# One pool of equal rooms in place of pools by phase, in a two-layer decoder trunk

## The chip, the core and the metric

The kernel runs on one core of a Trainium2 chip. The metric is the time of one execution in microseconds (us) on the device. TensorE (PE) multiplies matrices, VectorE (DVE), ScalarE (ACT) and GpSimd (POOL) work element by element, SyncE (SP) starts most DMA transfers. PE writes to eight PSUM banks of 512 float32 columns, which DVE and ACT empty.

## The reference

An input x of 1024 tokens by 1024 features goes through two layers and a last norm. In each layer:

- u = rms_norm(h), and one projection of u gives q, k, v and a forget logit for 8 attention heads of 64, and q, k, v and a gate for 8 retention heads.
- Attention: softmax of q k / 8 plus the differences of a running sum of log-sigmoid forget logits, causal, times v.
- Retention: rotary q and k, in chunks of 128 tokens with a decaying state, then a norm for each head, times silu of the gate.
- h += concat(attention, retention) @ w_out.
- h += (gelu(conv3(rms_norm(h) @ w_up_a)) * (rms_norm(h) @ w_up_g)) @ w_down, with 2816 inner features.
- h += sigmoid(rms_norm(h) @ w_gate) * (p @ w_proj).

## The kernel before

All activations lie with features on the 128 partitions and the 1024 tokens along the free axis, so a tile is 128 x 1024 float32, 4 KB a partition. To keep float32 accuracy each operand is cut into a high and a low part (`split`, lines 111 to 117: a ScalarE cast and a subtraction on VectorE or GpSimd), and every product is three matmuls.

The program builder traces instructions in program order; a scheduler then orders each engine's queue by a simulated time, program order being the priority. So matmuls of different products may be mixed wherever their inputs are ready in the simulation. On the chip each queue runs in its order.

**Attention stage** (lines 758 to 898). Weights come through `load_w` (load, cast, subtract) with two buffers for each of its three tiles; `weights()` always fetches one more before it hands one out, so two are ahead. `weave` (line 843) mixes a chain of dense projections (`DENSE`) with units of attention and retention head pairs, each paced between two positions of the dense chain (`SPANS`). The last retention pair is paced between 251.1 and 259.3, over the embedding's projection (`g_embed`), the last of the chain. Each retention pair leaves two `turn`s (transposes into `mixed`) for later; those of the last pair come behind the weave.

**Matrix stages** (lines 901 to 1032). The out-projection, the up- and down-projection and the gate use a seven-product scheme for a 2 x 2 block product: `parts` (line 334) runs the products b0, a, b1, c1, b2, c2, b3 with three matmuls of 512 columns for each moving pair. b0, b1, b2 and b3 gather in one PSUM bank, c1 and c2 in another, a in a third, and between products of one bank the bank is read (`join`, `form`). `Moving` (line 215) holds the moving side of a pair of tiles in seven tiles: its sums and their splits. `Fixed` (line 259) holds the weight side, built in four steps beside the part before. A stage's norm is not applied ahead: `Stats` adds up squares, `finish` sums them with 16 small matmuls (line 404) and spreads the result with matmuls of line 418, and the result scales the products.

Phases follow each other through `turn_to`, which closes all tile pools of a phase and opens those of the next; a few tiles (`mh`, `ssq`, `rc`, `rb`) live across. In the matrix phase a tag has a fixed number of buffers: `mh` 9, `c` 2, `x` 28, `wr` 4, `ws` 2, `wh` 4, `wl` 3, and all 8 banks are one ring. Borders that matter here:

- All four `Moving` of the mixed heads are built at the start of the matrix phase (line 925), after all attention and retention. The out-projection has two halves of four `parts`, first on attention heads, then on retention heads; in the second half the u of the next stage is built from each finished pair of h (line 936).
- Up to down: the results z and their sums go to DRAM (`zd`), since all come back in groups of three or two (`GROUPS`). The reloaded tiles `zz` use two buffers of tag `c` and one of `mh` (lines 986 to 998).
- In the gate, tiles `sg` use the two buffers of `c`; each is last used as the room for a square (line 1031). Behind it layer 1 opens its pools, fetches two weights and builds eight u (lines 1034 to 1037).
- The last layer's gate runs in a stage of its own (lines 1039 to 1091), with u built at line 1042.

Of the kernel before, what the change touches and what calls it, by code (L numbers as in the profile page):

```python
# [17 lines left out]
DEPTH = 2  # L18
D = 1024
T = 1024  # L20
# [11 lines left out]
FVW = 264  # L32


DENSE = ("fi1", "fi2", "fv1", "fi3", "rv0", "ri0", "rv1", "rg0", "ri1", "ri2", "rg1", "ri3", "ep0", "em0")
SPANS = ((6, 42.6), (42.6, 79.9), (85.9, 123.5), (130.4, 145.5), (138.9, 199.2), (194.7, 197.7), (217.3, 254.5), (251.1, 259.3))

TURNS = (1, 2)
PIECES = ((0, 512), (512, 512))
# [21 lines left out]

@with_exitstack
def trunk(ctx, tc, ap):
    nc = tc.nc
    const = ctx.enter_context(tc.tile_pool(name="const", bufs=1))
    keep = ctx.enter_context(tc.tile_pool(name="keep", bufs=1))
    dr = ctx.enter_context(tc.tile_pool(name="dr", bufs=2, space=DRAM))

# [4 lines left out]
    BUFS = dict(st=6, tp=5, L=4, c=2, u=16, mh=9, ssq=1, x=28, wr=4, ws=2, wh=4, wl=3)  # L73
    KEPT = ("mh", "ssq")
    sb = ps = banks = None

    @contextmanager
    def phase(name):

        nonlocal sb, ps, banks  # L80
        banks = 8 if name[:3] == "ffn" else 4
        with ExitStack() as stack:
            sb = stack.enter_context(tc.tile_pool(name="sb_" + name, bufs=1, reuse_waits="tile"))
            ps = stack.enter_context(tc.tile_pool(name="ps_" + name, bufs=1, space=PSUM, reuse_waits="tile"))
            yield

    def G(tag, name, dt=F32, shape=(P, T)):
        return (keep if tag in KEPT else sb).tile(list(shape), dt, name=name, tag=tag, bufs=BUFS[tag])

# [3 lines left out]
    def spsum():  # L93
        return ps.tile([P, 512], F32, name="s", tag="s", bufs=banks)

    def bank():
        return ps.tile([P, 512], F32, name="q", tag="s", bufs=banks)

    def hb(name, dt=F32):
        return sb.tile([P, 512], dt, name=name, tag="hb", bufs=6)  # L100

    def small(name, shape, dt=F32, bufs=2):
        return (keep if name == "rc" else sb).tile(list(shape), dt, name=name, tag=name, bufs=bufs)
# [16 lines left out]
    def load_w(src, kk, width, eng):  # L120
        raw = sb.tile([P, kk, width], F32, name="wr", tag="wr", bufs=2)
        nc.sync.dma_start(raw, src)
        hi = sb.tile([P, kk, width], F32R, name="wh", tag="wh", bufs=2)
        lo = sb.tile([P, kk, width], F32R, name="wl", tag="wl", bufs=2)
        split(hi, lo, raw, eng)
        return hi, lo

    def weight_order():
        V, G_ = nc.vector, nc.gpsimd
        for l in range(DEPTH):  # L130
            qk = lambda j: (ap["wqk"][l, j], KC, P, E("qk", j))
            tm = lambda j: [(ap["wtm"][l, j, i], 4, 256, E("tm", 2 * j + i)) for i in range(2)]
            fv0 = [(ap["wfv"][l][i], 4, FVW, G_) for i in range(2)]
            specs = {"ep": lambda i: [],
# [6 lines left out]
            yield from (None, None)  # L141
# [11 lines left out]
    def weights():  # L153
        fetch()
        return ahead.pop(0)
# [30 lines left out]
    def g_dense_tm(x, evac):  # L186
# [3 lines left out]
        for i in range(2):  # L190
            hi, lo = weights()
# [9 lines left out]
    def dense_tm_wide(x, width, evac):  # L201
        w0 = weights()
        w1 = weights()
        for b in range(NB):
            if b % 2 == 0:
                d = dpsum()
            o = d[:, (b % 2) * 512:(b % 2) * 512 + width]
            for k in range(KC):
                hi, lo = (w0, w1)[k // 4]
                mm_tm(o, x, b, k, hi[:, k % 4, :], lo[:, k % 4, :], k == 0, k == KC - 1)  # L210
            evac(b, o)

    class Moving:


        def __init__(self, a, b, scales=None, ta=None, tb=None):

            a1, b1, b2 = a[:, 0:512], b[:, 0:512], b[:, 512:T]  # L220
            if ta is None:
                ta, tb = sums(a, b, scales)
            self.x = []
            for n, (src, scale) in enumerate(((a[:, 0:512], scales and scales[0]), (b[:, 0:T], scales and scales[1]),
                                              (ta.rearrange("p c t -> p (c t)"), None), (tb.rearrange("p c t -> p (c t)"), None))):
                if n == 0:
                    t = G("x", "xs", F32R, (P, 2, 512))
                    hi, lo = t[:, 0, :], t[:, 1, :]
                else:
                    hi, lo = G("x", "xh", F32R), G("x", "xl", F32R)  # L230
                if scale is None:
                    split(hi, lo, src)
                else:
                    split_scaled(hi, lo, src, scale)
                self.x.append((hi, lo))

        def of(self, part):
            n, slot = ((0, 0), (1, 0), (2, 0), (2, 1), (3, 0), (1, 1), (3, 1))[part]
            return [v[:, slot * 512:(slot + 1) * 512] for v in self.x[n]]

    def sums(a, b, scales=None):

        a1, a2, b1, b2 = a[:, 0:512], a[:, 512:T], b[:, 0:512], b[:, 512:T]
        ta, tb = G("c", "ta", F32, (P, 2, 512)), G("c", "tb", F32, (P, 2, 512))
        t2, t1, t3, t4 = ta[:, 0, :], ta[:, 1, :], tb[:, 0, :], tb[:, 1, :]
        if scales:
            sa, sbb, sn = scales
            nc.scalar.activation(t3, a2, AF.Copy, scale=sa)
            nc.vector.scalar_tensor_tensor(t1, a1, sa, t3, op0=ALU.mult, op1=ALU.subtract)
            nc.vector.scalar_tensor_tensor(t3, b2, sbb, t3, op0=ALU.mult, op1=ALU.subtract)  # L250
        else:
            sn = -1.0
            nc.vector.tensor_tensor(t1, a1, a2, op=ALU.subtract)
            nc.vector.tensor_tensor(t3, b2, a2, op=ALU.subtract)
        nc.vector.scalar_tensor_tensor(t2, b2, sn, t1, op0=ALU.mult, op1=ALU.subtract)
        nc.vector.scalar_tensor_tensor(t4, b1, sn, t2, op0=ALU.mult, op1=ALU.subtract)
        return ta, tb

    class Fixed:


        def __init__(self, src, n, loads):

            self.n, self.w = n, n * P
            self.raw = []
            for i in range(2):
                t = G("wr", "wr", F32, (P, 2, self.w))
                loads.append(nc.sync.dma_start(t, src[i]))
                self.raw.append(t)
            self.x = []  # L270
            self.todo = [self.first, self.second, self.third, self.fourth]

        def step(self):
            if self.todo:
                self.todo.pop(0)()

        def split(self, t, c=2):
            if c == 2:
                hi, lo = G("wh", "wh", F32R, (P, 2, self.w)), G("wl", "wl", F32R, (P, 2, self.w))
            else:  # L280
                both = G("wh", "wb", F32R, (P, 2, self.w))
                hi, lo = both[:, 0:1, :], both[:, 1:2, :]
            nc.scalar.copy(hi, t)  # L283
            nc.vector.tensor_tensor(lo, t, hi.bitcast(F32), op=ALU.subtract)  # L284
            self.x.append((hi, lo))

        def first(self):
            self.split(self.raw[0])

        def second(self):  # L290
            (a, b), s = self.raw, G("ws", "ws", F32, (P, 2, self.w))
            nc.gpsimd.tensor_tensor(s[:, 1, :], b[:, 0, :], b[:, 1, :], op=ALU.add)  # L292
            nc.gpsimd.tensor_tensor(s[:, 0, :], s[:, 1, :], a[:, 0, :], op=ALU.add)
            self.p = s
            self.split(s)

        def third(self):
            (a, b), s = self.raw, G("ws", "ws", F32, (P, 2, self.w))
            nc.gpsimd.tensor_tensor(s[:, 0, :], b[:, 0, :], a[:, 0, :], op=ALU.add)  # L299
            nc.gpsimd.tensor_tensor(s[:, 1, :], self.p[:, 0, :], a[:, 1, :], op=ALU.add)  # L300
            self.split(s)

        def fourth(self):
            self.split(self.raw[1][:, 1:2, :], 1)

        def of(self, part, p):
            n, slot = ((0, 0), (0, 1), (1, 0), (1, 1), (2, 0), (2, 1), (3, 0))[part]
            return [v[:, slot, p * P:(p + 1) * P] for v in self.x[n]]

    class Line:  # L310


        def __init__(self, specs):
            self.specs = iter(specs)
            self.loads = []
# [3 lines left out]
        def load(self):  # L319
            spec = next(self.specs, None)  # L320
            self.ahead = spec and Fixed(*spec, self.loads)

        def take(self):
            now = self.ahead
            while now.todo:
# [8 lines left out]
    def parts(line, moving, evac):  # L334

        w = line.take()
        b, c = bank(), None
        for part, name in enumerate(("b0", "a", "b1", "c1", "b2", "c2", "b3")):
            if name == "a":
                o = bank()  # L340
            elif name == "c1":
                o = c = bank()
            else:
                o = c if name == "c2" else b
            more = name in ("b1", "b2", "b3", "c2")
            for p, x in enumerate(moving):
# [5 lines left out]
                nc.tensor.matmul(o, wlo, xhi, start=False, stop=last, skip_group_check=more)  # L352
            evac(name, o)
            if part in (1, 3, 5, 6):
# [815 lines left out]
```

## Time and profile before

| | |
|---|---|
| median of 3 runs | 2930.85 us (2926.9 to 2933.22) |
| the profiled execution | 2932.09 us |
| its span, first to last instruction | 2930.3 us |
| PE, DVE, ACT, POOL busy | 92%, 71%, 42%, 31% of the span |
| mean granted clock of PE | 0.958 |
| DMA queue of SP | 302.42 MB, 32.5% of 16 engines |

A busy share is over the whole span. The granted clock is 1.00 where PE runs at 2.4 GHz and 0.50 where it runs at 1.2 GHz. In lists of waits, "X <- Y: a, n, b" means that X waited for Y a us in n waits, the longest of b.

### The profile page before, as it was taken

Reading aid. Unit: us, or ns where it says so; the run is one execution under the profiler, and the core shown is the slowest. Engines: PE = TensorE matmul, PEld = TensorE weight load, DVE = VectorE, ACT = ScalarE, POOL = GpSimd, SP = SyncE. Lnnn points to the kernel's source line nnn. Section 1 sums busy time; section 2 is a strip of 40 time slices with the busy share of each in tenths; the row PEclk is TensorE's granted clock in tenths of the full one; section 3 lists DMA queues with packets and bytes.
Section 4 is the critical chain, followed back from the end, with each engine's and each line's share of the span. In section 5 each row is a group of like instructions: output and inputs, shape, how many; then the busy total and the mean of one; then the engine's idle time right before and its main releaser. Section 6 shows DMA issues by size and latency. Waiting matters only on the chain. (4 is left out here: it accounts for less than half of the span.)

```text
span 2930.3 us, 36348 instructions
## 1 busy us (share of the span) xinstructions
PE 2699.2 (92%) x13718; PEld 2272.5 (78%) x13718; DVE 2085.0 (71%) x2991; ACT 1216.3 (42%) x1778; POOL 918.5 (31%) x650
## 2 busy tenths in 40 slices
PE   9999999779999988996889998997889999979998
PEld 8888888658888866784678888896678888758877
DVE  5566655797888876877545656566978888857777
ACT  4455523444433433433334555334434334333343
POOL 2222332343333331332332222323433333313321
PEclk9999999989999998998999999998989999979999
DMA  5234221431333345521242332213322233364334
GB/s 173 74 86 110 59 68 57 137 119 66 114 115 115 115 152 169 161 82 51 93 120 86 87 89 72 61 54 137 121 81 103 102 106 115 139 196 144 110 97 137
DMA packets 107937, 313.14 MB, mean 107 GB/s; under 512 B 12529, under 2 KB 33521, under 8 KB 107761
## 3 DMA queue, kind: packets, MB, share of 16 engines
q1 hardware_dynamic: 104688, 302.42, 32.5%
q10 hardware_dynamic: 3072, 8.39, 1.2%
q8 instruction: 108, 1.77, 0.3%
q14 instruction: 69, 0.56, 0.1%
HBM read 205.84 MB, written 71.37 MB: 95 GB/s over the span
## 5 line engine op out<-in xcount | busy, mean ns | idle before, releaser
L350 PE MATMUL q<-xh,wh 128*128 128x512 f32 x1560 | 617.3, 398 | 30.6 <-DVE h L362 16.4
L351 PE MATMUL q<-xl,wh 128*128 128x512 f32 x1560 | 615.1, 394 | 3.9 <-DVE xl L113 3.9
L352 PE MATMUL q<-xh,wl 128*128 128x512 f32 x1560 | 604.6, 394 | 0.0
L350 PEld LDWEIGHTS q<-xh,wh 128*128 128x128 f32 x1560 | 297.4, 191 | 112.3 <-DVE h L362 26.2
L292 POOL TENSOR_TENSOR ws<-wr 128x512 f32<-128x512 f32 (+2 forms) x96 | 143.4, 1494 | 715.5 <-DVE wl L284 596.2
L351 PEld LDWEIGHTS q<-xl,wh 128*128 128x128 f32 x1560 | 296.9, 190 | 69.7 <-DVE xl L113 9.5
L352 PEld LDWEIGHTS q<-xh,wl 128*128 128x128 f32 x1560 | 297.1, 190 | 62.4 <-DVE wl L284 0.6
L283 ACT CAST wh<-ws 128x1024 fp32r<-128x1024 f32 (+2 forms) x192 | 170.8, 891 | 367.1 <-PE q L351 165.9
L362 DVE TENSOR_TENSOR h<-h,q 128x512 f32<-128x512 f32 x336 | 225.2, 679 | 69.1 <-PE q L352 67.0
L182 PE MATMUL d<-wh,uh 128*128 128x256 f32 (+1 forms) x768 | 223.2, 291 | 11.8 <-DVE ks L508 8.6
L284 DVE TENSOR_TENSOR wl<-ws,wh 128x1024 fp32r<-128x1024 f32 (+2 forms) x192 | 198.8, 1035 | 33.5 <-ACT wh L283 33.4
L183 PE MATMUL d<-wl,uh 128*128 128x256 f32 (+1 forms) x768 | 220.9, 288 | 0.1
L184 PE MATMUL d<-wh,ul 128*128 128x256 f32 (+1 forms) x768 | 219.8, 287 | 0.0
L299 POOL TENSOR_TENSOR ws<-wr 128x512 f32<-128x512 f32 (+2 forms) x96 | 121.8, 1269 | 308.7 <-DVE wl L284 308.7
L113 POOL TENSOR_TENSOR wl<-wr,wh 128x1024 fp32r<-128x1024 f32 (+1 forms) x49 | 119.7, 2445 | 270.9 <-ACT wh L112 179.6
L350 PE MATMUL q<-xs,wh 128*128 128x512 f32 x312 | 128.9, 413 | 46.9 <-ACT xs L112 34.9
L524 POOL TENSOR_TENSOR yb<-yb,triangle 128x128 f32<-128x128 f32 x128 | 67.2, 527 | 334.5 <-DVE mn L539 259.1
L162 PE MATMUL d<-uh,wh 128*128 128x512 f32 x512 | 166.7, 403 | 1.1 <-ACT wh L112 0.7
L162 PE MATMUL d<-ul,wh 128*128 128x512 f32 x512 | 163.4, 396 | 0.6 <-DVE ul L117 0.6
L164 PE MATMUL d<-uh,wl 128*128 128x512 f32 x512 | 161.3, 395 | 2.7 <-POOL wl L113 2.5
L182 PEld LDWEIGHTS d<-wh,uh 128*128 128x128 f32 x768 | 147.6, 192 | 16.3 <-DVE ks L508 10.3
L300 POOL TENSOR_TENSOR ws<-ws,wr 128x512 f32<-128x512 f32 (+2 forms) x96 | 156.3, 1628 | 0.2
(248 smaller groups left out, 6170.6 us busy)
## 6 DMA issues: line engine op xcount, KB each, us to landing
wr<-in_wup_dram SPq DMA_DIRECT2D x88, 512.0 KB, 3.7
zz<-zd SPq DMA_DIRECT2D x66, 512.0 KB, 3.7
zd<-z SPq DMA_DIRECT2D x44, 512.0 KB, 3.6
wr<-in_wdown_dram SPq DMA_DIRECT2D x48, 384.0 KB, 4.0
wr<-in_wqk_dram SPq DMA_DIRECT2D x32, 512.0 KB, 3.5
zd<-ta SPq DMA_DIRECT2D x22, 512.0 KB, 2.6
zd<-tb SPq DMA_DIRECT2D x22, 512.0 KB, 4.7
wr<-in_wtm_dram SPq DMA_DIRECT2D x20, 512.0 KB, 3.8
```

Of the source, the lines that this page charges most:

```text
L162: nc.tensor.matmul(outs[h], whi, x[:, h * 512:(h + 1) * 512], start=s, stop=False)
L164: nc.tensor.matmul(outs[h], wlo, xhi[:, h * 512:(h + 1) * 512], start=False, stop=stop)
L182: nc.tensor.matmul(o, x[k][0][:, tok], hi, start=start, stop=False)
L183: nc.tensor.matmul(o, x[k][0][:, tok], lo, start=False, stop=False)
L184: nc.tensor.matmul(o, x[k][1][:, tok], hi, start=False, stop=stop)
L283: nc.scalar.copy(hi, t)
L284: nc.vector.tensor_tensor(lo, t, hi.bitcast(F32), op=ALU.subtract)
L300: nc.gpsimd.tensor_tensor(s[:, 1, :], self.p[:, 0, :], a[:, 1, :], op=ALU.add)
L350: nc.tensor.matmul(o, whi, xhi, start=first, stop=False, skip_group_check=more)
L351: nc.tensor.matmul(o, whi, xlo, start=False, stop=False, skip_group_check=more)
L352: nc.tensor.matmul(o, wlo, xhi, start=False, stop=last, skip_group_check=more)
L362: nc.vector.tensor_tensor(dst, dst, s, op=op)
```

## The change

- All tile pools of phases go. One pool holds 50 rooms of 4 KB and 6 of 2 KB (`Arena`). Each tile takes, in program order, the room that has been free for longest, and gives it back when the program drops its last reference. The first use of a room's new tile is ordered behind the first use of its tile before.
- `Moving` and `Fixed` are cut into four stages (products b0; b1, c1; b2, c2; a, b3). The order of the products becomes b0, b1, c1, b2, c2, a, b3. After each stage `after(n)` may drop that stage of the old moving side and build the same stage of the next. `Joined` builds from two tiles, `Stored` from DRAM, whose load runs one stage ahead.
- The seven products use one of two double banks for b and c, and one of four single banks for a, in all stages.
- The first half of the out-projection (`g_out`) becomes the last member of the dense chain (`wo0`); the last retention pair is paced between 251.1 and 300.0.
- `finish` is called in product a, the sixth, and the scaling of c22 and of the first tile stands there.
- h goes to DRAM before the gate and is loaded again there part by part; u of layer 1 is built during the gate's last part.
- `weights()` fetches only when fewer than two are ahead; the first value weights come in three tiles of at most three blocks.

The same sums are computed; the diff, cut to its core:

```diff
+class Arena:
+    def take(self, name, dt, shape):
+        free = self.free[T if int(np.prod(shape[1:])) > T // 2 else T // 2] or self.free[T]
+        room = Room(self, free.popleft(), name)
+        return Part(self.pool.tile(list(shape), dt, name=name, tag=room.place, bufs=1), room)
...
-SPANS = (..., (251.1, 259.3))
+SPANS = (..., (251.1, 300.0))
...
     def weights():
-        fetch()
+        if len(ahead) < 2:
+            fetch()
...
+    NAMES = ("b0", "b1", "c1", "b2", "c2", "a", "b3")
...
+    class Stored(Moving):
+        def load(self, n):
+            self.raw[n] = G("zz", F32, (P, 512 if n == 0 else T))
+            nc.sync.dma_start(self.raw[n], self.src[n][:, 0:512 if n == 0 else T])
+        def fill(self, n, hi, lo):
+            raw, self.raw[n] = self.raw[n], None
+            split(hi, lo, raw if n == 0 else raw.rearrange("p (c t) -> p c t", c=2))
...
+    def g_parts(line, moving, evac, after=None):
         w = line.take()
-        b, c = bank(), None
+        d = dpsum()
...
+            o = spsum() if name == "a" else d[:, 512:T] if name[0] == "c" else d[:, 0:512]
...
             evac(name, o)
-            if part in (1, 3, 5, 6):
+            if part % 2 == 0:
+                w.x[part // 2] = None
+                if after:
+                    after(part // 2)
                 line.step()
+            yield 0.7 * len(moving)
...
+        def g_out():
+            line = Line(specs())
+            for p in range(2):
+                mx.append(Joined(mixed[2 * p], mixed[2 * p + 1]))
+            for q in range(4):
+                for m in (2 * q, 2 * q + 1):
+                    h[m] = G("h")
+                    nc.sync.dma_start(h[m], h_dram[m])
+                to = h[2 * q:2 * q + 2]
+                yield from g_parts(line, mx, lambda name, s: join(name, s, to))
...
+            def after(n):                      # last up part
+                for m in u:
+                    m.drop(n)
+                for m in stored[0]:
+                    m.build(n)
+                    if n < 3:
+                        m.load(n + 1)
...
+                def after(n):                  # last gate part
+                    for m in old:
+                        m.drop(n)
+                    if n:
+                        u.extend(make_u(h[m], nw[:, 2 * NW_ATTN + l + 1, m:m + 1]) for m in (2 * n - 2, 2 * n - 1))
```

## Rows read from the trace of the kernel before

**Rows 1.** The page's engine totals: busy us, share of span, instructions.
```profile
PE 2699.2 (92%) x13718; PEld 2272.5 (78%) x13718; DVE 2085.0 (71%) x2991; ACT 1216.3 (42%) x1778; POOL 918.5 (31%) x650
```
**Rows 2.** Windows: us; busy PE, PEld, DVE, ACT, POOL (instructions); clock, DMA share, GB/s.
```profile
50.00:500.00 450.00, 435.25 (x2867) 393.16 (x2866) 264.09 (x611) 199.69 (x384) 122.56 (x107) 0.99 0.30 78
535.00:670.00 135.00, 101.31 (x390) 76.27 (x390) 129.12 (x171) 62.87 (x85) 59.14 (x42) 0.86 0.37 121
750.00:1050.00 300.00, 300.00 (x1325) 248.43 (x1325) 246.97 (x237) 119.46 (x143) 111.70 (x62) 1.00 0.32 112
1083.00:1133.00 50.00, 27.16 (x70) 17.35 (x71) 27.86 (x31) 14.54 (x18) 3.70 (x4) 0.66 0.73 239
1310.00:1372.00 62.00, 33.12 (x131) 25.66 (x130) 59.44 (x65) 30.51 (x37) 25.22 (x14) 0.78 0.20 60
1372.00:1490.00 118.00, 93.64 (x381) 74.84 (x380) 63.60 (x60) 46.46 (x54) 38.88 (x18) 0.88 0.29 96
2013.00:2148.00 135.00, 103.16 (x395) 77.43 (x396) 129.44 (x171) 62.99 (x85) 59.39 (x42) 0.85 0.35 114
2563.00:2613.00 50.00, 28.83 (x78) 18.85 (x79) 26.30 (x30) 16.19 (x19) 4.69 (x4) 0.66 0.72 239
2800.00:2830.00 30.00, 24.86 (x96) 20.19 (x95) 25.89 (x26) 15.37 (x16) 8.57 (x3) 0.83 0.30 96
```
**Rows 3.** Timeline of PE, 1355 to 1373: start, us, instruction, idle before.
```profile
1361.37 3.58 PE L404 MATMUL s<-ones,ssq 128*128 128x1 f32 x16 [11.67 <-DVE ssq L395]
1368.64 3.79 PE L418 MATMUL s<-ident,rc 128*128 128x128 f32 x16 [3.70 <-POOL rc L407]
```
**Rows 4.** Waits of PE, 500 to 700.
```profile
PE s L404 <- DVE ssq L395: 7.8, 1, 7.8
PE s L733 <- DVE yn L728: 7.1, 1, 7.1
```
**Rows 5.** Waits of PE, 1083 to 1133.
```profile
PE q L350 <- ACT xs L112: 17.4, 3, 13.0
```
**Rows 6.** Waits of ACT, 1083 to 1133.
```profile
ACT xh L112 <- DMA zz<-zd: 14.8, 7, 4.6
ACT xs L112 <- DMA zz<-zd: 11.8, 1, 11.8
```
**Rows 7.** Groups of DVE, 530 to 670: count, busy us, mean ns, idle before.
```profile
L362 DVE TENSOR_TENSOR h<-h,q 128x512 f32<-128x512 f32 x56 | 37.1, 674 | 0.8 <-PE q L352 0.5
L284 DVE TENSOR_TENSOR wl<-ws,wh 128x512 fp32r<-128x512 f32 x16 | 11.0, 690 | 0.0
L113 DVE TENSOR_TENSOR xl<-ta,xh 128x1024 fp32r<-128x1024 f32 x8 | 9.7, 1212 | 0.3 <-ACT xh L112 0.3
L253 DVE TENSOR_TENSOR ta<-mixed 128x512 f32<-128x512 f32 x4 | 3.2, 808 | 0.0
```
**Rows 8.** Waits of PE, 1300 to 1500.
```profile
PE s L404 <- DVE fr L488: 9.0, 1, 9.0
PE q L350 <- ACT sg L368: 6.6, 2, 6.4
```
**Rows 9.** DMA issues: count, KB each, median us from issue to landing.
```profile
zz<-zd SPq DMA_DIRECT2D x66, 512.0 KB, 3.7
```
**Rows 10.** Groups over the whole span, shapes kept apart.
```profile
L113 POOL TENSOR_TENSOR wl<-wr,wh 128x1024 fp32r<-128x1024 f32 x45 | 109.9, 2444 | 232.9 <-ACT wh L112 159.6 <-issue 73.1
...
L113 DVE TENSOR_TENSOR xl<-zz,xh 128x1024 fp32r<-128x1024 f32 x66 | 86.9, 1320 | 36.4 <-ACT xh L112 36.4
...
L112 ACT CAST wh<-wr 128x1024 fp32r<-128x1024 f32 x72 | 75.4, 1047 | 143.9 <-PE d L162 97.3 <-issue 20.5 <-PE s L1074 9.1
...
L368 ACT COPY a<-q 128x512 f32<-128x512 f32 x44 | 25.8, 586 | 77.9 <-PE q L352 77.9
...
L1029 POOL TENSOR_TENSOR sg<-sg,ppt 128x1024 f32<-128x1024 f32 x8 | 20.1, 2510 | 48.3 <-ACT sg L1028 44.4 <-DMA ppt<-pp 3.9
```
**Rows 11.** Waits of PE, 50 to 500.
```profile
PE d L164 <- POOL wl L113: 1.3, 1, 1.3
```

More of the change, by code (lines that the diff above doesn't have):

```diff
@@ new lines, with __init__, __del__, back @@
+class Room:
+    __slots__ = ("arena", "place", "name", "used")
+    def __init__(self, arena, place, name):
+        self.arena, self.place, self.name, self.used = arena, place, name, False
+    def __del__(self):
+        self.arena.back(self)
+class Arena:
+    def __init__(self, tc, pool, whole, half):
+        self.tc, self.pool = tc, pool
+        self.free = {T: deque("m%d" % i for i in range(whole)), T // 2: deque("n%d" % i for i in range(half))}
+        self.taken = []
+        self.first = {}
+    def back(self, room):
+        self.taken.remove(room.name)
+        self.free[T if room.place[0] == "m" else T // 2].append(room.place)
+    def take(self, name, dt, shape):
+        free = self.free[T if int(np.prod(shape[1:])) > T // 2 else T // 2] or self.free[T]
+        if not free:
+            raise MemoryError("no room left for %s: %s" % (name, ", ".join(sorted(self.taken))))
+        room = Room(self, free.popleft(), name)
+        self.taken.append(name)
+        return Part(self.pool.tile(list(shape), dt, name=name, tag=room.place, bufs=1), room)
+    def use(self, room, ins):
+        if room.used:
+            return
+        room.used = True
+        before = self.first.get(room.place)
+        if before is not None and before is not ins:
+            self.tc.add_manual_dep(ins, before.name, mybir.DependencyInfo(mybir.DependencyClass.NoSync, mybir.DependencyReason.DATA),
+                                   reason="order of rooms")
+        self.first[room.place] = ins
@@ L290, in second @@
[L290 to L301, printed above, removed]
@@ L320, in load @@
             spec = next(self.specs, None)
-            self.ahead = spec and Fixed(*spec, self.loads)
+            self.ahead = spec and Fixed(*spec)
         def take(self):
             now = self.ahead
-            while now.todo:
+            while now.done < 4:
                 now.step()
@@ L563, in scores @@
             if q == 1:
-                t = [G("L", "L") for _ in range(self.room)]
+                t = [G("L") for _ in range(self.room)]
                 if self.room == 1:
@@ L922, in trunk, with scales @@
+        units += [(a, e, 12.5, lambda i=i: ret(i)) for i, (a, e) in enumerate(SPANS[4:])]
+        weave(chain(*(makers[d[:2]](int(d[2])) for d in DENSE)), units)
+        while tail:
+            tail.pop(0)()
+        ret_v.clear()
+        del vst[:]
+        def scales(which, p):
+            return nw[:, which, 2 * p:2 * p + 1], nw[:, which, 2 * p + 1:2 * p + 2], minus[:, which, 2 * p + 1:2 * p + 2]
         stats = Stats()
+        mx = [Joined(mixed[2 * p], mixed[2 * p + 1]) for p in (2, 3)]
@@ new lines, in trunk @@
+            z = [G("z") for i in range(2)]
+            if last:
+                rb = None
+                for m in stored[0]:
+                    m.load(0)
+            def after(n):
+                for m in u:
+                    m.drop(n)
+                for m in stored[0]:
+                    m.build(n)
+                    if n < 3:
+                        m.load(n + 1)
+            parts(line, u, lambda name, s: form(name, s, z, lambda i: act[i]), after if last else None)
+            act = body = None
@@ L1003, in trunk, with after @@
-                if group is GROUPS[-1]:
-                    if l + 1 < DEPTH:
-                        u.append(Moving(*to, scales(2 * NW_PLE + l, q)))
-                    for m in (2 * q, 2 * q + 1):
-                        stats.add(h[m], G("mh", "hsq"), None, E("hsq", m))
-        if l + 1 < DEPTH:
-            _, rb = stats.finish()
+                if q == 3:
+                    for m in then:
+                        m.load(0)
+                def after(n):
+                    for m in mx:
+                        m.drop(n)
+                    for m in then:
+                        m.build(n)
+                        if n < 3:
+                            m.load(n + 1)
+                    if not then and not ends:
+                        u[2].build(n)
@@ new lines, in trunk @@
+                parts(line, mx, lambda name, s: join(name, s, to), after if q == 3 else None)
+                if not then:
+                    if ends:
+                        u += [make_u(h[m], nw[:, 2 * NW_PLE + l, m:m + 1]) for m in (2 * q, 2 * q + 1)]
+                    else:
+                        u.append(Joined(*to, scales(2 * NW_PLE + l, q), q != 2))
+                    for m in (2 * q, 2 * q + 1):
+                        stats.add(h[m], G("hsq"), None, E("hsq", m))
+                        if not ends:
+                            nc.sync.dma_start(hs_dram[m], h[m])
```

569 lines of the change are left out of this document (319 added, 250 removed).

## The prediction, made before the changed kernel ran

> **What bounds the kernel now.** I read the engine totals of the page first, then the table of windows, then who PE waits for in the bad stretches, then the groups of the engine that is full there. TensorE is busy 92% of the span, VectorE 71% [rows 1]. The reader is to see that this average hides two kinds of stretch. In the up-projection PE never stops: 1325 matmuls in 300 us, 0.2264 us each, clock 1.00, VectorE 82% busy [rows 2]. The other rows of that table are the borders between stages. I price each as its length, less its wide matmuls at 0.2264 us, less what belongs to a norm's sum: 32 small matmuls in two groups of 16, 3.6 and 3.8 us at this clock [rows 3], call it 7.
>
> - A0, attention to up-projection: 135 - 358 x 0.2264 - 7 = 47 us lost; A1, the same in layer 1: 135 - 363 x 0.2264 - 7 = 46.
> - B0 and B1, up to down: 50 - 70 x 0.2264 = 34, and 50 - 78 x 0.2264 = 32.
> - C0, the last group of the down-projection: 62 - 99 x 0.2264 - 7 = 33. G, the gate: 118 - 349 x 0.2264 - 7 = 32.
> - C1, down to the last stage: 30 - 80 x 0.2264 - 3.6 = 8.
>
> Together 232 us of a 2930.3 us span, the half-speed clock of these rows (0.66 to 0.88) included [rows 2]. That is the purse the change can draw on. What ends the waits differs. In A and C VectorE is full: 129.1 of 135 and 59.4 of 62 us [rows 2]. In B both are idle and ScalarE waits for reloaded tiles: 11.8 us for the first, 14.8 for seven others [rows 6], while PE waits 17.4 us for the split of the first [rows 5]. In G nothing is full: the gate's tiles have two buffers, and the next part's first copy waits for the chain of sigmoid, GpSimd multiply, add and square that ends on them.
>
> **Part by part.** Durations are those of the profiled execution, which took 2932.1 us, 1.8 over its span and 1.2 above the median of 2930.85.
>
> *First half of the out-projection into the weave (A0, A1).* Before, no mixed tile is split until the last retention pair is done; PE even stands 7.1 us for that pair's last transposes [rows 4]. After, four `parts` on the attention heads (168 matmuls x 0.2264 = 38.0 us) run beside the last retention pair, whose pacing ends before them. VectorE's work that leaves the full stretch: 28 joins x 0.674 = 18.9; four weight sets, 4 x 4 x 0.690 = 11.0; two `Joined` at 3 x 1.212 + 5 x 0.808 = 7.7 each, 15.4 [rows 7]. A third `Joined`, of retention pairs long finished, can hide under the same matmuls: 7.7. Left are 129.1 - 45.3 - 7.7 = 76.1 us of VectorE, so the stretch becomes 38.0 + 76.1 = 114 against 135: 21 saved. What is late next is VectorE again: joins, u splits and squares of the second half are all still there, so most of the 47 is not won. Against the 21 stands that VectorE must take 45 us more during about 75 us of PE work, for which I take off 4. Value 17 each; bounds 0 (VectorE late in the weave by all of it) and 47. The eight weight loads and eight h loads that move go past the stores of the embedding on SP's queue, with the DMA engines 37% busy in the old place [rows 2]; they are needed one part at a time, so I cost them at nothing, and 3.7 us each [rows 9] if one is late.
>
> *Sum of squares asked for at the sixth product instead of the first.* PE's queue stands 7.8 us at A0 and 11.7 us at C0 on VectorE's last square [rows 3, 4]. After, five products of 12 matmuls (13.6 us) go ahead. At A this is the same VectorE backlog that I have counted, so nothing more. At C0 no work leaves VectorE, and this plus building stage 0 of u first is the whole gain: value 12, bounds 0 and 33.
>
> *Stored stages at the up/down border (B0, B1).* Each of the last part's stages is dropped, a stage of the first group is built from a tile loaded one stage earlier, and the next load goes out. The building is 3 x (0.72 + 3 x 1.32) = 14 us on VectorE [rows 10], the half-wide split taken at 0.72, about half,, in a part of 84 x 0.2264 = 19 us with 18% of VectorE free; the backlog of some 10 us is worked off while the first down parts (63 matmuls, 14 us) ask less of it. The loads of a stage are three of 512 KB, 3.7 us [rows 9]: 4 to 11 us, as they overlap or not, against 5.4 us of PE per stage. If they do not overlap, three stages lose 5.7 each, 17 us. I take 7 lost, nearer to overlap, since B0 already moved 239 GB/s [rows 2]. Value 27 each; bounds 15 and 34. The other groups' borders work alike and cost nothing visible before or, I assume, after.
>
> *Gate.* The rooms are no longer two, so four parts of 19 us run on. Of its loss, 9.0 us stand at the entry to layer 1 behind a first instruction in newly opened pools, 6.6 behind copies into the two tiles [rows 8]. The chain of the last quarter stays: evacuation, sigmoid, 2.5 us on GpSimd [rows 10], add, split. Six of eight u pairs are built earlier, six steps of the first chunk, so it is mostly covered. The 8 added stores and 8 loads of h are 16 x 3.7 us on DMA engines that are 29% busy. Value 24; bounds 0 and 32.
>
> *Last stage's entry (C1).* u is built part by part: 5, bounds 0 and 8.
>
> *Order of products and banks.* Products b0 and b1 now follow each other in one bank, so b1 must wait for b0's evacuation: 0.586 us of copy [rows 10] plus the tail. Product c1 uses the other bank and the same stage, and the trace shows matmuls of different products mixed in time, so it can stand between. I charge 0.1 us for each of 96 calls, 10 us. Bounds: 0, and 96 x 0.8 = 77 us if nothing stands between.
>
> On this point the Trainium skill, "Perfetto Trace Analysis", section "Optimizing Tensor Performance", says that independent matmul groups should rotate through different PSUM banks so that the evacuation of one overlaps the matmuls of the next. The order before obeys it with product a between; the new one does not within b0 and b1, and by the rule alone the dearer bound would hold. The trace before has no such adjacency, so no row decides.
>
> *One pool of 50 rooms and 6 halves, weight look-ahead one instead of two.* Each new tile takes the room freed longest ago. In attention I count nearly all rooms taken, so a load can start only when a room just used is free. PE now waits 1.3 us in 450 for a weight split [rows 11]: the cover is good. I cost it at nothing; if cover is gone a weight tile of 512 KB costs its load (taken at that of zz), cast and GpSimd split, 3.7 + 1.05 + 2.44 = 7.2 us [rows 9, 10]. Better placing could win some of the 14.8 us that PE idles in 450 us of attention [rows 2]; I take no gain.
>
> Sum: 2 x 17 + 12 + 2 x 27 + 24 + 5 - 10 = 119. 2932.1 - 119 = 2813, and 1.2 less beside the median: **2812 us**.
>
> **Rivals.**
> 1. *The borders nearly vanish.* The weave absorbs the splits, u stages replace each other without a backlog, and 85% of the 232 us goes: 2734. For: VectorE is busy only 264 of 450 us in the attention stage [rows 2]. Against: A and C are full of VectorE work that the change moves only in part.
> 2. *A new wait at the border eats half.* Either the shared bank costs its 77 us (2932 - 129 + 77 = 2880), or VectorE and reloads hold A, B and C as before and only the gate and half of B come: about 50, 2881. For: VectorE at 96% in A and C. Against: the free order of matmuls, and B's idle engines. The page's rule on banks above speaks for the first.
> 3. *Slower: rooms run short.* With one pool in program order, weight tiles in the attention stages and the last stage (78 of them: 31 a layer and 16) are loaded into rooms that matmuls have only just left, and PE waits for the whole 7.2 us. It decides from 119 / 7.2 = 17 tiles; at 30 tiles 2932 - 119 + 216 = 3029. For: few rooms free in attention. Against: before, buffers for weights were two deep too, with 1.3 us of waiting, and in the last stage half the rooms are empty.
>
> The Trainium skill, "Perfetto Trace Analysis", section "Optimization Strategy", has a rule on the same mechanism: a gap that repeats on the engine that should be full can mean too little room for the next tile. Before, the trace shows none in the up-projection, 300.00 of 300 us busy [rows 2]; by the rule, such gaps after the change would be rival 3, and the 3029 is its time.
>
> 4. *The shared pool changes nothing that counts*, gains and new waits cancelling: 2931.
>
> **How the numbers follow.** Chances: forecast 0.52, rival 1 0.16, rival 2 0.16, rival 3 0.12, rival 4 0.04. The forecast's own range is 2770 to 2855. The range for 8 in 10 takes in rival 2 and most of rival 1: 2720 to 2900. A difference under 0.2% (about 6 us) cannot be told from none; faster by more is 0.52 + 0.16 + 0.16 = 0.84, the same 0.04, slower 0.12.
>
> **What would show it.** Right: wide matmuls of the out-projection among the last retention pair's, and the stretch from there to the up-projection still full on VectorE; PE nearly unbroken from up into down; no PE wait on squares; gate and entry to layer 1 about 25 us shorter. Wrong: gaps that repeat in the up-projection after each first product (rival 2), or PE waits on weight splits summing to tens of us in attention (rival 3). If VectorE is not full in A after the change, my main bound is wrong and rival 1 is nearer.

## The result, and the profile after

The changed kernel takes **3070.69 us** (median of 4 runs, 3068.28 to 3072.66) against 2932.03 of the kernel before, run beside it: ratio 1.0476, 95% interval 1.0458 to 1.0494. It is slower by 139 us where 119 us of gain were forecast, and outside the range.

In the trace after, every instruction has one line (L145, the wrapper that records them), so tiles tell what it is. First the engine totals of the page, to set beside [rows 1]:

```profile
PE 2772.6 (90%) x13718; PEld 2279.6 (74%) x13718; DVE 2123.8 (69%) x3031; ACT 1222.9 (40%) x1822; POOL 910.9 (30%) x652
```

Then the windows, columns as in [rows 2]: attention, the stretch A0, the inside of the up-projection in layer 0, B0, the same two of layer 1.

```profile
50.00:500.00 450.00, 423.36 (x2770) 385.65 (x2769) 245.73 (x591) 195.82 (x379) 114.52 (x104) 0.97 0.28 74
545.00:700.00 155.00, 122.95 (x525) 92.40 (x524) 133.74 (x199) 66.87 (x100) 48.26 (x39) 0.92 0.24 82
750.00:1050.00 300.00, 277.95 (x1172) 220.95 (x1171) 226.31 (x210) 104.93 (x126) 96.68 (x56) 0.99 0.28 97
1130.00:1180.00 50.00, 36.63 (x131) 27.50 (x130) 40.95 (x43) 21.07 (x25) 16.59 (x10) 0.88 0.61 208
...
2300.00:2600.00 300.00, 282.10 (x1160) 221.44 (x1159) 229.72 (x208) 103.88 (x126) 102.69 (x56) 0.97 0.29 96
2670.00:2720.00 50.00, 36.36 (x137) 27.60 (x136) 42.35 (x42) 20.92 (x25) 14.04 (x10) 0.86 0.68 220
```

The reader is to see where the loss is: not at a border, but inside the up-projection, which had no gap before. It now runs 1172 matmuls in 300 us, not 1325, and VectorE is not the cause, 75% busy against 82%. The border B0 did gain: 50 - 131 x 0.2264 = 20 us lost, 34 before; B1 50 - 137 x 0.2264 = 19, 32 before. These 50 us don't hold all of the border after: over 150 us around it (1033 to 1183 and 2513 to 2663 before, with 510 and 508 matmuls; 1080 to 1230 and 2620 to 2770 after, with 540 and 527) the loss falls only from 35 to 28 and from 35 to 31, of which the longer step told of below hides some 3.

For the whole span I gave each of the 13718 matmuls the time to the start of the next one, and summed by the stage that it belongs to, so a wait at a border counts to the stage ahead of it (us, from the profiled execution of each; first line the sum before, then differences to it; names of experiments as below):

| | attention | out | up | down | gate, last | norms | all |
|---|---|---|---|---|---|---|---|
| before | 1078.5 | 209.7 | 892.8 | 494.5 | 199.9 | 47.5 | 2922.8 |
| after | +22.9 | +16.0 | +89.8 | +17.5 | +4.6 | -14.6 | +136.2 |
| e1, alternate | +19.3 | +12.0 | +42.5 | +5.9 | -2.4 | -15.8 | +61.6 |
| e4, 4K | +27.6 | +13.7 | +80.7 | +9.0 | +4.8 | -13.6 | +122.3 |
| e14, ring | +12.4 | +6.1 | +66.6 | +7.2 | -1.1 | -16.5 | +74.7 |
| e16, ring, 4K | +18.0 | +5.4 | +54.2 | +7.9 | -5.6 | -14.6 | +65.3 |
| e15, ring, 4K, alternate | +10.8 | +7.2 | +21.6 | -7.0 | +0.4 | -15.3 | +17.7 |
| e7, before, order | -2.2 | +4.4 | +2.7 | -1.6 | -2.6 | -0.9 | -0.2 |
| e13, before, pairs | -2.8 | +23.7 | +144.0 | +25.8 | +21.1 | -5.6 | +206.2 |
| e11, rooms held | +14.4 | +14.4 | +166.8 | +9.4 | -5.3 | -14.6 | +185.1 |
| e2, own raw rooms | +59.7 | +21.7 | +66.2 | +18.1 | +7.3 | -10.5 | +162.6 |

Who PE waits for inside the up-projection, 750 to 1050 (nobody before):

```profile
PE d L145 <- ACT a L145: 13.8, 7, 2.5
PE d L145 <- DVE a L145: 8.2, 7, 1.2
```

PE waits for the copies that empty b. Who ScalarE waits for there:

```profile
ACT w L145 <- DMA wr<-in_wup_dram: 23.9, 14, 3.4
```

and SyncE's queue, which starts the loads:

```profile
SPq L145 <- PE d L145: 106.7, 8, 13.4
```

The timeline shows both in one gap (start, us, instruction, idle before):

```profile
983.86 0.62 ACT L145 CAST w<-wr 128x512 fp32r<-128x512 f32 x1 [2.63 <-DMA wr<-in_wup_dram]
984.39 0.58 ACT L145 COPY a<-d 128x512 f32<-128x512 f32 x1
...
985.02 0.50 PE L145 MATMUL d<-xh,wh 128*128 128x512 f32 x1 [1.72 <-ACT a L145]
```

ScalarE, in order, stands 2.63 us on a weight load; the copy of b0 is behind it, and b1, which goes to the same bank, behind the copy. The 8.2 us are of another kind: there b0's first matmul waits for the last read of the pair that the part two before has used.

### The profile page after: what moved, and what is told of

Read it like the earlier page. It is cut to its first block, busy times and chain, and to the rows that moved or that the text cites. A ratio compares the mean times of both kernels' runs of the same rounds, so it can differ in the third digit from the quotient of the medians.

```text
span 3067.4 us, 36378 instructions
## 1 busy us (share of the span) xinstructions
PE 2772.6 (90%) x13718; PEld 2279.6 (74%) x13718; DVE 2123.8 (69%) x3031; ACT 1222.9 (40%) x1822; POOL 910.9 (30%) x652
## 4 chain that ended last, share of the span: by engine, by line
PE 59%; DVE 14%; DMA 11%; POOL 7%; issue 5%; ACT 4%; SPq 1%; ACTq 0%; POOLq 0%; DVEq 0%
PE d L145 45%; PE s L145 14%; POOL ws L145 6%; DMA wr<-in_wup_dram 4%; DVE xl L145 2%; DVE wl L145 2%; DVE h L145 2%; DMA wr<-in_wdown_dram 1%; DVE t L145 1%; DVE conv L145 1%; DMA sw<-raw 1%; DVE ssq L145 1%; SPq L145 1%; DMA yb<-cum_rows 1%; DMA wr<-in_wqk_dram 1%
## 5 line engine op out<-in xcount | busy, mean ns | idle before, releaser
L145 PE MATMUL d<-xh,wh 128*128 128x512 f32 x1560 | 643.4, 413 | 109.6 <-DVE h L145 40.6
L145 POOL TENSOR_TENSOR ws<-wr 128x512 f32<-128x512 f32 (+2 forms) x192 | 272.7, 1428 | 1277.1 <-PE d L145 443.6
L145 PE MATMUL d<-xh,wl 128*128 128x512 f32 x1560 | 628.3, 404 | 3.4 <-DVE wl L145 3.4
L145 PE MATMUL d<-xl,wh 128*128 128x512 f32 x1560 | 629.7, 404 | 1.7 <-DVE xl L145 1.7
L145 PEld LDWEIGHTS d<-xh,wh 128*128 128x128 f32 x1560 | 302.6, 194 | 225.8 <-DVE h L145 43.0
L145 PEld LDWEIGHTS d<-xh,wl 128*128 128x128 f32 x1560 | 302.4, 194 | 76.5 <-DVE wl L145 4.8
L145 PEld LDWEIGHTS d<-xl,wh 128*128 128x128 f32 x1560 | 302.8, 194 | 68.7 <-DVE xl L145 2.5
L145 PE MATMUL d<-x,w 128*128 128x512 f32 x936 | 253.5, 413 | 61.2 <-ACT w L145 26.6
L145 POOL TENSOR_TENSOR ws<-ws,wr 128x512 f32<-128x512 f32 (+2 forms) x192 | 290.1, 1512 | 8.1
L145 ACT CAST wh<-ws 128x1024 fp32r<-128x1024 f32 (+2 forms) x192 | 170.0, 886 | 266.0 <-POOL ws L145 259.6
L145 PEld LDWEIGHTS d<-x,w 128*128 128x128 f32 x936 | 178.7, 195 | 119.4 <-ACT w L145 35.3
L145 DVE TENSOR_TENSOR h<-h,d 128x512 f32<-128x512 f32 x288 | 195.6, 682 | 93.4 <-PE d L145 92.0
L145 DVE TENSOR_TENSOR wl<-ws,wh 128x1024 fp32r<-128x1024 f32 (+2 forms) x192 | 219.8, 1146 | 55.5 <-ACT wh L145 47.0
L145 ACT CAST wh<-wr 128x1024 fp32r<-128x1024 f32 (+4 forms) x174 | 164.8, 948 | 233.3 <-DMA wr<-in_wqk_dram 55.7
L145 PE MATMUL d<-wh,uh 128*128 128x256 f32 (+1 forms) x768 | 222.3, 291 | 12.6 <-ACT wh L145 6.7
L145 PE MATMUL d<-wl,uh 128*128 128x256 f32 (+1 forms) x768 | 222.4, 290 | 1.2 <-DVE wl L145 1.2
L145 PE MATMUL d<-wh,ul 128*128 128x256 f32 (+1 forms) x768 | 221.8, 290 | 0.0
L145 PE MATMUL d<-uh,wh 128*128 128x512 f32 (+1 forms) x584 | 194.9, 403 | 19.0 <-DVE flog L145 10.0
L145 POOL TENSOR_TENSOR wl<-wr,wh 128x1024 fp32r<-128x1024 f32 (+2 forms) x51 | 126.9, 2491 | 245.9 <-ACT wh L145 206.5
L145 PE MATMUL d<-ul,wh 128*128 128x512 f32 (+1 forms) x584 | 193.1, 397 | 1.6 <-DVE ul L145 1.6
L145 PE MATMUL d<-uh,wl 128*128 128x512 f32 (+1 forms) x584 | 189.6, 394 | 0.4 <-POOL wl L145 0.3
L145 DVE TENSOR_TENSOR wl<-wr,wh 128x1024 fp32r<-128x1024 f32 (+2 forms) x123 | 150.9, 1227 | 39.7 <-ACT wh L145 27.9
```

The costliest lines, as they stand in the source:

```text
L145: ins = f(*[bare(v) for v in a], **{n: bare(v) for n, v in k.items()})
```

## The experiments

Three theories for the up-projection. **S**: b0 and b1 share a bank and follow each other. **R**: with two double banks a part's banks come back after two parts, and both together; before, eight single banks, three a part, came back after 8/3. **W**: a room hands to its next tile the wait for the last user of an unrelated one. Apart from these **L**: 512-column matmuls follow each other at 226.7 to 227.2 ns in the up, down, gate and last stages before and at 231.4 to 231.9 after (means of the steps under 260 ns), and the addresses of their tiles make it.

**e1** alternates the banks:

```diff
-    NAMES = ("b0", "b1", "c1", "b2", "c2", "a", "b3")
+    NAMES = ("b0", "c1", "b1", "c2", "b2", "a", "b3")
```

> The changed kernel with the products in the order b0, c1, b1, c2, b2, a, b3, so that no two products of one bank follow each other in program order; stages, rooms and banks as they are. Theory S (shared bank): in the two up-projections of the changed kernel the excess over 0.2264 us a matmul is 64 and 70 us against 25 and 25 before, most of it at the first matmul of b1 and b2; it goes, and the time falls from 3071 by 60 to 80 us, to about 3000. Theory W (weights late): ScalarE stands on a weight load (24 and 15 us in two stretches) ahead of the copies that PE waits for; the order of products doesn't touch that, so at least two thirds of the gaps stay: over 3045 us. Theory R (too few double banks): a part still holds its two banks for as long, no change: 3060 to 3075 us.

2999.73 us, ratio 1.0236 [1.0212, 1.0259]: 71 less than the change. The time is S's, but S isn't shown: see e7, and the rows of e13, by which the alternating order doesn't free a product from the one ahead of it.

**e2** keeps four rooms for raw weights.

```diff
+        if name == "wr" and self.raw or not free:
+            free = self.raw                     # four of the 50 rooms
```

> The changed kernel with four of the 50 rooms kept for raw weights (wr), so that a weight load waits for the split of an old raw tile and not for matmuls that read some other tile of that room. Theory W: SyncE's waits on PE (107 us in 330 us of the up-projection) and ScalarE's on the loads go, and with them 40 to 70 us: 3000 to 3030 us. Theory S: the gaps at b1 and b2 stay: 3060 to 3075 us. With four rooms fewer for the rest the attention stages may lose up to 10 us under either.

3093.95 us, 1.0551 [1.0533, 1.0570]: slower. The loads are early now, but the wait only went to the next tile: in 750 to 1050 ScalarE's splits wait for the stores of z that lived in their rooms.

```profile
ACT wh L149 <- DMA zd<-z: 61.5, 7, 8.8
```

The up-projections gain 24 us; attention loses 37, with four rooms fewer for all else.

**e3** takes a third pair of banks:

```diff
+        third = turn_of[0] % 3 == 0             # every third part
+        b, c = (spsum(), None) if third else (d[:, 0:512], d[:, 512:T])
```

> The changed kernel with every third part's b and c in two single banks, so that a bank comes back after three parts and not after two. Theory R: the waits at the first matmul of b0 (14 and 4 us in the two up-projections) go and PE's order loosens: 3035 to 3055 us. Theories S and W: 3060 to 3075 us.

3053.87 us, 1.0413 [1.0391, 1.0435]: 17 less. R's range, but every third part is then without a pair as well, which the rows of e13 make a rival.

**e4** moves the rooms from 4000 + 4096 i and beyond, with small tiles between, to 4064 + 4096 i, where the tiles of the matrix stages lay before.

```diff
+    pad = const.tile([P, 16], F32, name="pad")  # 64 B; small tiles go to a pool of their own
```

> The changed kernel with all 50 rooms moved to addresses that lie like the tiles of the matrix stages before (64 B further, and the small tiles out from between the rooms). Theory L (place): the step from one 512-column matmul to the next, 231.8 ns in the changed kernel's matrix stages, falls to the 227 ns of before; some 6,900 such steps x 4.9 ns = 34 us: 3037 us. If the place doesn't matter: 3066 to 3075 us and 231 to 232 ns.

3050.87 us, 1.0412 [1.0396, 1.0427]. L holds: the step is 227.2 to 228.6 ns in up, down, gate and last. A stretch of the last stage without a gap, first of the kernel after, then of e4; 197 matmuls lie in 45 us of the one and 200 in the other, with some two in each that reach in from outside:

```profile
2980.00:3025.00 45.00, 45.00 (x197) 36.53 (x196) 30.00 (x43) 17.30 (x25) 2.42 (x1) 1.00 0.30 93
```

```profile
2966.00:3011.00 45.00, 45.00 (x200) 37.25 (x199) 29.98 (x44) 17.37 (x25) 2.41 (x1) 1.00 0.28 90
```

Only 20 of the 34 us come; where PE waits for others, a faster step waits longer.

**e5** lets a tile prefer a room of its own kind.

```diff
+        place = next((p for p in free if self.held.get(p) == kind), free[0])
```

> The changed kernel, but a tile takes the longest free room that last held a tile of its own kind (raw weights, their sums, their splits, all else), and only without one the longest free of all. Theory W (a room hands over the waits of an unrelated tile: SyncE's weight loads wait for matmuls, 107 us in 330, ScalarE's splits for loads and stores): these waits go and the up-projections' 42 and 47 us above before shrink by half: 3015 to 3035 us. If the shared bank alone makes the gaps: 3055 to 3075 us.

3107.61 us, 1.0602 [1.0584, 1.0620], a miss. In 750 to 1050 SyncE's loads no longer wait for PE, but for the making of earlier weights, as they would where a room of the own kind was given back too recently:

```profile
SPq L151 <- DVE wl L151: 110.4, 14, 16.2
```

**e8** put this beside e1 and e4:

> The changed kernel with the alternating order of the first experiment, the room addresses of the fourth and the rooms by kind. If the three add up (71, 20 and 15 to 25 us): 2955 to 2965 us, the up-projections within 15 us of before, and what is left above 2931 is attention and the out-projection. If rooms by kind win nothing: about 2980 us.

3093.26 us, 1.0559 [1.0543, 1.0575]: a miss; that the reason is the same isn't shown.

**e6** undoes the move of the first half of the out-projection.

```diff
-DENSE = (..., "ep0", "em0", "wo0")
+DENSE = (..., "ep0", "em0")
```

> The changed kernel with the first half of the out-projection taken out of the weave again, behind all attention and retention, and the last retention pair paced to 259.3 as before. If the move pays what was forecast (17 us a layer): 3071 + 34 = 3105 us. If it only moves VectorE's work into a stage that is short of rooms (out-projection 9 and 7 us, attention 9 and 14 us dearer than before): 3030 to 3060 us.

3091.23 us, 1.0545 [1.0530, 1.0561]: the move pays, 20.5 us.

**e7** takes the order alone into the kernel before.

```diff
-        for part, name in enumerate(("b0", "a", "b1", "c1", "b2", "c2", "b3")):
+        for part, name in enumerate(("b0", "b1", "c1", "b2", "c2", "a", "b3")):
```

> The kernel before with one thing of the change alone: the products in the order b0, b1, c1, b2, c2, a, b3 (the scaling of the first tile moves from c2 to a); pools, the ring of eight banks and all else as before. Theory S, adjacency alone is the price: 40 to 77 us, 2970 to 3008 us. If it takes the two double banks or late weights as well: within 10 us of 2931.

2933.28 us, 1.0009 [1.0000, 1.0019]. S alone falls: the order costs at most 6 us here. **e13** takes the banks alone, **e9** both:

```diff
-        b, c = bank(), None
+        d = dpsum()                             # one of two; four single banks for a
+        b, c = d[:, 0:512], d[:, 512:T]
```

> The kernel before with the banks of the change alone (b and c in one of two double banks, a in one of four single banks), products in the order of before. The ninth experiment lost 213 us with banks and order together, the seventh 2 us with the order alone. If the banks alone are the price: over 3100 us. If it takes both, order and banks: 2930 to 2960 us.

> The kernel before with the order of the products and the banks of the change (b and c in one of two double banks, a in one of four single banks); pools of tiles by phase stay. Theory S with R (the shared bank costs only where a part's banks come back after two parts): the up-projections lose what the alternating order won back, 40 to 70 us: 2970 to 3000 us. Theory W (the one pool of rooms makes the weights and the copies late, and the order of the products only lends them slack): within 12 us of 2931.

e13: 3138.23 us, 1.0703 [1.0687, 1.0718]; e9: 3142.60, 1.0726 [1.0711, 1.0740], over 140 us more than either theory gave it. So the pairs alone are a price, with pools by phase and the order of before. The window of e13, then PE's waits and ScalarE's in it:

```profile
750.00:1050.00 300.00, 269.48 (x1138) 214.91 (x1139) 203.50 (x206) 103.10 (x124) 73.09 (x54) 0.98 0.29 94
```

```profile
PE d L349 <- ACT wh L283: 14.4, 7, 2.1
PE d L349 <- ACT z L369: 10.2, 7, 1.5
```

```profile
ACT wh L283 <- PE d L350: 67.6, 20, 6.9
```

Of 20 parts inside the up-projection ten wait at the first matmul of b0, 22.2 us, ten at that of b2, 16.2, and ten at that of b3, 9.4. The rows show a circle: PE waits for ScalarE's copies out of the banks and for splits of weights, and these splits wait for PE to be done with older weights. All engines fall back together, VectorE to 68%.

b0 waits for a weight split, not for a bank. The waits of b2 and b3 are none that S or R foresaw: b2 goes to b's bank, but starts 0.05 us after the copy of c1 (L369) out of the other bank of the pair; L374 then reads b2.

```profile
853.19 0.59 ACT L369 ACTIVATE z<-d 128x512 f32<-128x512 f32 x1
853.83 0.50 PE L349 MATMUL d<-xh,wh 128*128 128x512 f32 x1 [1.46 <-ACT z L369]
856.88 0.69 DVE L374 TENSOR_TENSOR z<-z,d 128x512 f32<-128x512 f32 x1 [0.63 <-PE d L351]
```

A pair is one tile of the program, and a product in one half waits for the read of the other half ahead of it; call this **T**. Counted in the built programs, a product waits for a read of the other half 370 times in the changed kernel, 359 in e13, 338 in e1, and never in the kernel before. Whether the pairs cost more by T or by the later return (R) isn't settled: no run takes one without the other, and e3 lessens both.

**e14** gives the changed kernel a ring of eight, **e16** adds e4, **e15** adds e1 as well. Four of the eight banks are still the halves of two pairs, and in e14 a product still waits 137 times for a read of the other half:

```diff
+        if i > 3:                               # i counts banks taken, modulo 8
+            return spsum()
+        if i % 2 == 0:
+            ring[1] = dpsum()
+        return ring[1][:, i % 2 * 512:i % 2 * 512 + 512]
```

> The changed kernel with a part's three banks taken in turn from all eight, as before; the order of the products, the rooms and all else as in the change. If the banks with the order make most of the up-projections' loss: these 42 and 47 us fall under 15 each, about 3000 us. If the rooms make it (four withheld rooms cost 51 us): it stays over 3050 us.

> The changed kernel with the ring of eight banks and the rooms at the addresses of the fourth experiment, products in the order of the change. Ring alone gave 3011, ring, addresses and alternating order 2951 us. If the addresses give the 20 to 33 us of the spacing and the order the rest: 2978 to 2990 us. If with the ring the order gives nothing, as in the kernel before: 2945 to 2957 us.

> The changed kernel with the ring of eight banks, the alternating order and the rooms at the addresses of the fourth experiment. If the banks were the cause, the order has nothing more to mend and the addresses give 20 to 30 us: 2965 to 2980 us. If rooms are the cause, the result is near that of the first and fourth experiments together, 2980 us, with gaps left in the up-projections. If both shares add up: 2940 to 2960 us.

e14: 3010.58 us, 1.0270 [1.0255, 1.0285], 60 less than the change; but the up-projections give only 23 of it (+66.6, after +89.8), where they were to come under 15 us each, and the rest comes in all the other stages. e16: 2994.54, 1.0211 [1.0191, 1.0231], 16 less again. e15: 2951.07, 1.0072 [1.0052, 1.0091], 44 less again. Their windows 750 to 1050, e14, e16, e15:

```profile
750.00:1050.00 300.00, 283.93 (x1193) 226.13 (x1193) 228.35 (x214) 106.30 (x129) 94.61 (x55) 0.98 0.28 95
```

```profile
750.00:1050.00 300.00, 283.92 (x1208) 230.11 (x1207) 231.40 (x216) 108.66 (x131) 99.94 (x57) 0.97 0.28 97
```

```profile
750.00:1050.00 300.00, 289.93 (x1255) 236.59 (x1254) 244.55 (x227) 111.62 (x135) 96.76 (x58) 0.99 0.29 101
```

So with the ring the order costs 44 us in the changed kernel and 2 in the one before. I put that down to the rooms, which leave the copies less slack, but it isn't shown: the pairs left in the ring (T) are a rival that no run tests. In e16 splits still wait for stores of other tiles:

```profile
ACT wh L146 <- DMA zd<-t: 15.7, 5, 5.2
```

**e12** puts e1, e3 and e4 together:

> The changed kernel with the alternating order, the rooms at the addresses of the fourth experiment and every third part in single banks. If the three add up (71, 20 and 17 us): 2963 us. If the order and the third pair mend the same wait: about 2980 us. In neither case faster than before, since attention and the out-projection keep some 40 us.

3017.81 us, 1.0307 [1.0291, 1.0323], a miss: worse than e1 alone. Three pairs don't mend what the ring does, and the mends don't add up; that each makes the scheduler order the queues anew may be why, but isn't shown.

**e11** tests W from the other side.

```diff
+            if j == 1:
+                held = [arena.free[T].popleft() for _ in range(4)]
```

> The changed kernel with four free rooms withheld during the up-projections alone (from the second pair of parts to the last); in program order 7 to 14 of the 50 rooms are free there. Theory W: each tile takes a room given back more recently, the waits grow, and the up-projections lose 30 us or more: over 3100 us. Theory S: nothing changes, 3063 to 3078 us.

3122.11 us, 1.0659 [1.0642, 1.0675]: 51 slower: 77 more in the up-projections (+166.8, after +89.8), some 28 less elsewhere.

```profile
750.00:1050.00 300.00, 267.26 (x1084) 210.51 (x1082) 202.47 (x199) 98.22 (x118) 87.07 (x51) 0.95 0.27 89
```

**e10** takes the later sum alone into the kernel before, **e17** with the order and product a:

```diff
-                if rb is None:
+                if rb is None and name == "b2":
                     _, rb = stats.finish()
```

> The kernel before with one thing of the change alone: the sum of squares is asked for at the fifth product of a part instead of ahead of the first, in the up-projection and in the gate. The small matmuls of the norms took 47.5 us in all before and 32.9 in the changed kernel; if that gain belongs to this step: 10 to 15 us, 2916 to 2921 us. If VectorE's backlog only moves the wait to the next product: within 5 us of 2931.

> The kernel before with the order of the change and the sum of squares asked for at the sixth product, in a, as in the change; pools and the ring of eight stay. If asking one product later than in the tenth experiment covers more of VectorE's backlog: under 2908 us. If the tenth has all of it: 2910 to 2918 us.

e10: **2912.88 us**, 0.9941 [0.9929, 0.9954], faster than both kernels and the best of all runs. The sum of C0 in its trace, to set beside [rows 3], no longer waits for a square:

```profile
1357.58 3.57 PE L404 MATMUL s<-ones,ssq 128*128 128x1 f32 x16
1364.85 3.78 PE L418 MATMUL s<-ident,rc 128*128 128x128 f32 x16 [0.42 <-POOL rc L407]
```

e17: 2922.53 us, 0.9974 [0.9966, 0.9983]: a miss; one product later gives less.

## Why the prediction was wrong

**The step that failed: "Order of products and banks".** It let c1, which uses the other bank, "stand between" b0 and b1, and priced this one adjacency at 0.1 us a call, 10 us in all, 77 at most. In the changed kernel c1 can't stand there: b and c are halves of one tile, and c1 itself waits for the copy of b1 (in the part of the timeline above b0 starts at 977.52, b1 at 985.02, c1 at 991.17). By the runs that term is about 100: the banks 60 (e14), the order 44 (e15 against e16), and the banks alone 205 in the kernel before (e13). I looked for b0 and b1 in one bank, and neither saw that the halves of a pair hang on each other nor counted how many parts the banks hold. Rival 2 named the right sign that would show (gaps after a first product), with half the mechanism and too small a price. The Trainium skill, "Perfetto Trace Analysis", section "Matmul Optimizations", asks that all eight PSUM banks be used. The change had all eight in name; e13 shows that how they are tied and come round counts as much.

**"One pool of 50 rooms ... I cost it at nothing"** failed too. Up-projection: four rooms fewer cost 51 us (e11); the order costs in the changed kernel only (e7, e15), beside the rooms and the pairs. No run gave more rooms, so what the 50 cost isn't measured. Addresses: 16 to 20 us (e4, e16), a cost that I had not thought of. Attention is 23 us dearer; four rooms fewer cost 37 there (e2), so rooms are short, but that those 23 are theirs wasn't isolated. Part of the gaps is rival 3's mechanism, a load that comes late (ScalarE's 23.9 us), seen in the place where I said that PE had no gap, at about a third of its price per gap: waits of 1 to 2.5 us, not 7.2.

**A, 34 forecast.** The move is worth 20.5 (e6). The sum kept VectorE full over A0, and said that its main bound is wrong if it isn't: VectorE is 86% busy there, 96% before, and PE waits 17.3 us for it and 14.5 for ScalarE (545 to 700). So work left VectorE, but the 114 us that the sum gave the stretch don't follow from VectorE alone; rival 1, to which this sign pointed, didn't come either. And the out-projections are 16 us dearer than before, part of it the step of 232 ns and the pairs of banks (6 to 7 with ring and addresses).

**B, 54 forecast.** 14 and 13 us by the windows of 50 us, 7 and 4 over 150; in e15, with the step and the banks mended, 14 and 13 over 150 us too (571 and 566 matmuls in 1050 to 1200 and 2560 to 2710). So the replacing by stages gives half of its value at best, and leaves 20 us a border.

**Sum asked later, 12 forecast.** Right in the wait: what PE waits for squares (tile `ssq`, us and times; first before, then after) falls by 25 us, and the step by itself gives 16 us with the sum at the fifth product (e10), 7 at the sixth (e17). The -14.6 of the norms are not this wait, which counts to the stage ahead, but the small matmuls and the waits between their groups.

```profile
  DVE ssq L395: 29.0, 4
```

```profile
  DVE ssq L145: 3.8, 4
```

**Gate, 24 forecast.** Nothing came. The wait on the two tiles went, but other waits on the same chain stand in the gate, 1350 to 1560:

```profile
PE d L145 <- DVE h L145: 9.5, 4, 4.7
PE d L145 <- ACT sg L145: 9.2, 6, 3.7
```

**Last stage's entry, 5 forecast.** No run takes it alone; PE stands 3.9 us there between the two groups of the norm's sum, where it didn't stand before.

The gains seen (20 for A, 11 to 27 for B, 15 for the sums) are some 46 to 62 us of the 129 forecast; with a loss of 139 that means 185 to 200 us of costs. Banks, order and addresses are 120 of them, shown by e15, which is still 18 us slower than before: attention +10.8, out +7.2 and up +21.6, of this one wait of 17.2 us for a weight split at B1. What makes the 65 to 80 us that are left isn't settled beyond the signs for the rooms and the pairs left in the ring.

## What to carry to other kernels

Count after how many units of work a PSUM bank or a buffer comes back, and with what it is tied, not only how many there are, and look whether two banks that are one tile make products wait for each other's copies: eight single banks and two pairs with four singles are both eight banks, and differ by 205 us here. A shared pool saved nothing here where rooms were short: it let a load wait for an unrelated matmul, and in-order queues carried that wait to the copy that PE needed. Take a change apart: one of its steps alone, asking for a sum later, made the kernel before 16 us faster.

## What the runs showed of the hardware

The step of 512-column matmuls depends on where their tiles lie: about 227 ns with all at 4064 + 4096 i bytes, about 232 with tiles at 4000 + 4096 i and other offsets (e4, all else equal but the small tiles' place). Which property of the address does it isn't settled. The granted clock is 1.00 in both windows shown with e4.
